# A dense expert stage that accumulates over three chunks instead of two

## The chip, the cores and the metric

The kernel runs on one core of one Trainium2 chip. Its time is the device time of one execution in microseconds (us). Of several runs the median is given. A profiled execution gives a trace: the start and duration of the instructions of TensorE (PE), VectorE (DVE), ScalarE (ACT) and GpSimd (POOL), the issues of transfers on the queues of SyncE (SP) and POOL, and what ended the idle time before an instruction.

## The reference

One layer of a diffusion backbone: attention and a linear recurrence, and behind them a mixer that retrieves experts. There are 256 context and 1024 latent tokens of 1024 channels, that is two and eight tiles of 128 tokens. The mixer is what the change touches. For each token, 8 heads choose 16 of 16384 experts each; an expert is a row of a table u and a row of a table v, both 16384 x 1024, float32.

```python
eid = jnp.take_along_axis(cid, pos, axis=-1)          # 128 experts of each token
g = jax.nn.softmax(best, axis=-1)
u = jnp.take(u_tab, eid, axis=0)
act = jax.nn.gelu(jnp.einsum('td,thkd->thk', xb, u))
vv = jnp.take(v_tab, eid, axis=0)
return jnp.einsum('thk,thkd->td', (g * act), vv)
```

## The kernel before

**Two ways through the mixer.** Four token tiles (both context tiles, two latent ones) are *gathered*, in `mix`: for each of the 128 experts of a tile's tokens, an indirect transfer issued by POOL brings a 128 x 1024 tile of u rows, a different expert for each token (L830), and DVE multiplies it by the tokens and sums (L833); then, 16 at a time, the v rows are gathered (L841) and DVE adds them, weighted, to the tile's sum (L847). That is 1024 gathered rows of 512 KB, in the names of the trace `row`.

The other six latent tiles are *dense*, in `dense`: all 16384 experts are computed for them, in 128 chunks of 128 experts, with the gate `gts` zero where a token did not choose an expert. For a chunk, `experts_in` (L696) multiplies the chunk's u rows with the tokens. For precision both factors are split into a high and a low part and three products are summed (`split`, L134 and L135: ACT writes the high part, DVE subtracts; `mm3`, L138 to L140). So the names `uh`, `ul`, `vh`, `vl`, `ah`, `al`. A chunk has 48 such matmuls of 384 columns on PE; ACT applies the GELU and gives `a` (128 x 768). DVE multiplies `a` by the gate (L761) and splits it. Then `add` (L724) multiplies with the chunk's v rows: 36 matmuls of 512 columns. Two of the six token tiles keep their sums in PSUM through all chunks (`res`, 12 matmuls of a chunk). The other four share two rotating PSUM tiles (`rot`, 24 matmuls of a chunk): a rot tile takes the products of the chunks of one *group* for one token tile and one half of the channels, ACT copies it to `q` (L741), and DVE adds `q` to the sum in SBUF (L742). A group is `GROUP` chunks.

**Early chunks.** For 44 of the 128 chunks `a` is computed ahead of the dense stage and stored in DRAM (`ad`), and loaded back in it (L758); there `ul` is computed by POOL. The other 84, the full chunks, do their u products in the dense stage. Early chunks come in pairs, so that of six chunks mostly two are early and four full.

**What sets the order.** A scheduler fixes the order of instructions on every engine when the program is built. The products of a group are added (`add`) when the first chunk of the next group has been prepared (L766, L767). The gathered rows are woven in by a credit: `tick` is called with a number of microseconds behind certain DVE instructions, the credit grows by it, and for each `D_STEP` = 2.0 us of it one more row is taken from the gather work. `paced` places the DVE instruction of that row right behind the DVE instruction of the tick, so where credit is given decides which DVE instructions stand between which rows. In the dense stage `a` times the gate and the split of `a` give `T_MUL` = 2.0 us each, and a group's adds share a sum that depends on whether the chunks beside them are early (`E_US`) or full (`PE_US`). Rows rotate through `N_ROW` tiles plus, in the dense stage, `N_MORE` more; a gather into a tile waits until DVE has read the row before in it.

The helper `row()` takes the tiles in turn; `order` and `ahead` (L689, L690) are the groups and whether they are early.

Of the kernel before, what the change touches and what calls it, by code (L numbers as in the profile page):

```python
# [9 lines left out]
F32 = mybir.dt.float32  # L10
F32R = mybir.dt.float32r
# [4 lines left out]
AF = mybir.ActivationFunctionType  # L16
# [5 lines left out]
P = 128  # L22
D = 1024
KD = D // P
S_CTX = 256
# [21 lines left out]
N_RES = 2  # L47
GROUP = 2
EARLY = 44
N_ROW = 4  # L50
N_MORE = 3

# [3 lines left out]
T_MUL = 2.0  # L56
E_US = 3.0
PE_US = 15.8

# [5 lines left out]
def body(ctx: ExitStack, tc: tile.TileContext, i, o):  # L65
# [622 lines left out]

    order = [range(c, c + GROUP) for c in range(0, P, GROUP)]  # L689
    ahead = [n * (EARLY // GROUP) % len(order) < EARLY // GROUP for n in range(len(order))]  # L690
    early = [c for cs, e in zip(order, ahead) if e for c in cs]
    ad = {c: dram.tile([P, TD], F32, name=f"ad{c}") for c in early}
    nb = -(-TD // 512)
    NB = TD // nb

    def experts_in(raw, nraw, c, hh, hl, out):  # L696

        u = raw.tile([P, KD, P], F32, name="u", bufs=nraw)
        nc.sync.dma_start(u, i["ut"][c])
        uh = eu.tile([P, KD, P], F32R, name="uh", bufs=2)  # L700
        ul = eu.tile([P, KD, P], F32R, name="ul", bufs=2)
        split(uh, ul, u, G if c in early else V)
        for b in range(nb):
            bs = slice(b * NB, (b + 1) * NB)
            p = eps.tile([P, NB], F32, name="u", bufs=2)
            for k in range(KD):
                mm3(p, (uh[:, k], ul[:, k]), (hh[:, k, bs], hl[:, k, bs]), k == 0, k == KD - 1)
            out(bs, p)

    def dense(tiles, hh, hl):  # L710
        with ExitStack() as es:
# [11 lines left out]

            def add(group, full):  # L724
                c0 = group[0][0]
                share = GROUP * (PE_US - 2 * T_MUL if full else E_US)
                for it in group:
# [3 lines left out]
                for x in range(N_RES, N_DENSE):  # L731
                    for hf in range(2):
                        p = ps.tile([P, 512], F32, name="rot", bufs=2)
                        for it in group:
                            product(p, x, hf, it, c0, c0 + GROUP - 1)
                        y = acc[x - N_RES][:, hf * 512:(hf + 1) * 512]
# [7 lines left out]
            last = None  # L744
            for cs, taken in zip(order, ahead):
                group = []
                for c in cs:
# [5 lines left out]
                    if c % 2 == 0:  # L753
                        gts = wk.tile([P, TD, 2], F32, name="gt", bufs=2)
                        nc.sync.dma_start(gts, gd[c // 2])
                    a = wk.tile([P, TD], F32, name="a", bufs=2)
                    if taken:
                        nc.sync.dma_start(a, ad[c])  # L758
                    else:
                        experts_in(wk, 2, c, hh, hl, lambda bs, p: A.activation(a[:, bs], p, AF.Gelu_apprx_tanh))  # L760
                    tick(T_MUL, V.tensor_tensor(a, a, gts[:, :, c % 2], op=OP.mult))  # L761
                    ah = wk.tile([P, TD], F32R, name="ah", bufs=GROUP + 1)
                    al = wk.tile([P, TD], F32R, name="al", bufs=GROUP + 1)
                    tick(T_MUL, split(ah, al, a))
                    group.append((c, ah, al, vh, vl))
                    if last:  # L766
                        add(last, not taken)  # L767
                        last = None
                last = group
            add(last, True)  # L770
            more.clear()
# [84 lines left out]
    with ExitStack() as ms:  # L856
# [4 lines left out]
        ctab = load("ctab", [P, NC], dt=I32)  # L861
        kc = load("kcT", [P, S_CTX])
        maskb = load("maskb", [P, 2, P], dt=BF16)
# [53 lines left out]
    with ExitStack() as fs:  # L917
# [3 lines left out]
        with ExitStack() as ks:  # L921
            kv = pool(ks, "lkv")
            kT = kv.tile([P, S_LAT], F32, name="kT")
            vv = kv.tile([P, N_LAT, P], F32, name="vv")
# [51 lines left out]
    with ExitStack() as es:  # L976
# [17 lines left out]
        for c in early:  # L994
            def keep_act(bs, p):
                a = vl.tile([P, NB], F32, name="a", bufs=2)
                A.activation(a, p, AF.Gelu_apprx_tanh)  # L997
                nc.sync.dma_start(ad[c][:, bs], a)
            experts_in(vl, 1, c, hha, hla, keep_act)
        phase("chB")  # L1000
# [96 lines left out]
```

## Time and profile before

| | |
|---|---|
| median of 3 runs | 3699.52 us (3689.12 to 3724.33) |
| profiled execution | 3691.55 us, its span 3689.7 us |
| mean granted clock of TensorE | 0.951 of 2.4 GHz |
| busy, PE / DVE / ACT / POOL | 3323.2 / 3082.3 / 1456.6 / 1728.7 us |
| busy share of the span | 90% / 84% / 39% / 47% |
| moved by DMA | 918.20 MB, 249 GB/s over the span |

The busy time is the time in which an engine executes; a busy share is an average over stages with different limits. The dense stage takes some 1880 us, about from 1760 to 3650 us of the span; ahead of it lie the modulation, the input projection, attention and recurrence, the output projection, the choice of experts, and the early chunks. A PE instruction's duration in the trace overlaps the next one's, so the distance of the starts is the time that one takes of the engine; for DVE the distance is some 0.08 us shorter than the duration.

### The profile page before, as it was taken

What the parts mean: (1) busy time and instruction counts of PE and PEld (TensorE: products, weight loads), DVE (VectorE), ACT (ScalarE), POOL (GpSimd) and SP (SyncE); (2) the same over time, 40 slices, a digit from 0 to 9 for tenths busy, and PEclk for the clock granted to TensorE, in tenths of its full rate; (3) what the DMA queues carried; (4) which work ended last, traced back from release to release, by engine and by line L of the source; (5) the groups of instructions that cost most, each with busy time, mean ns of one, the idle gap of its engine ahead of it and who ended that gap; (6) DMA issues with size and microseconds to landing.
All of it is one profiled execution on the core that took longest, in us unless ns stands there. A gap on an engine that the chain in (4) does not pass through costs nothing.

```text
span 3689.7 us, 48648 instructions
## 1 busy us (share of the span) xinstructions
PE 3323.2 (90%) x16982; PEld 2733.0 (74%) x16982; DVE 3082.3 (84%) x6710; ACT 1456.6 (39%) x2270; POOL 1728.7 (47%) x1162
## 2 busy tenths in 40 slices
PE   7888879888798988889899999989989999999995
PEld 4477654433598877779788888878878888887884
DVE  4549986767799999970699999989989998988898
ACT  5744645533211344542333333433333333333333
POOL 0012454556621121212366666656657666665663
PEclk8799989999899999999999999999999999999998
DMA  8342653568830256773799999988889998988885
GB/s 333 109 158 84 211 201 127 159 233 283 287 97 28 66 152 203 215 218 125 278 346 331 339 341 337 337 307 317 319 300 343 349 344 303 343 303 308 302 317 200
DMA packets 349142, 918.20 MB, mean 249 GB/s; under 512 B 29144, under 2 KB 150104, under 8 KB 345824
## 3 DMA queue, kind: packets, MB, share of 16 engines
q0 software_dynamic: 147456, 536.94, 41.3%
q1 hardware_dynamic: 201440, 378.16, 30.1%
q8 instruction: 133, 2.18, 0.2%
q14 instruction: 113, 0.93, 0.1%
HBM read 834.48 MB, written 80.50 MB: 248 GB/s over the span
## 4 chain that ended last, share of the span: by engine, by line
PE 33%; DVE 24%; issue 6%; DMA 3%; POOL 2%; ACT 1%; POOLq 0%; DVEq 0%; SPq 0%; ACTq 0%
PE u L140 6%; PE u L139 6%; PE u L138 6%; DVE row L833 4%; DVE acc L847 4%; PE rot L138 3%; PE rot L140 3%; PE rot L139 3%; DVE acc L742 2%; DVE oh L676 2%; PE res L138 2%; PE res L140 2%; PE res L139 2%; DVE oh L674 1%; DVE oh L677 1%
## 5 line engine op out<-in xcount | busy, mean ns | idle before, releaser
L830 POOL DMA_INDIRECT row<-in_peer_u,eid x512 | 732.6, 1431 | 571.1 <-DVE row L833 219.0
L841 POOL DMA_INDIRECT row<-in_peer_v,eid x512 | 716.3, 1399 | 493.1 <-DVE acc L847 226.9
L140 PE MATMUL u<-hh,ul 128*128 128x384 f32 x2048 | 709.2, 347 | 59.0 <-DVE ul L135 55.7
L138 PE MATMUL u<-hh,uh 128*128 128x384 f32 x2048 | 709.9, 347 | 6.2 <-ACT a L997 4.4
L139 PE MATMUL u<-hl,uh 128*128 128x384 f32 x2048 | 708.1, 346 | 0.0
L847 DVE SCALAR_TENSOR_TENSOR acc<-row,w,acc 128x1024 f32<-128x1024 f32 x508 | 655.9, 1291 | 25.8 <-DMA row<-in_peer_v,eid 24.3
L833 DVE SCALAR_TENSOR_TENSOR row<-row,h 128x1024 f32<-128x1024 f32 x512 | 623.9, 1233 | 56.6 <-DMA row<-in_peer_u,eid 56.4
L741 ACT ACTIVATE q<-rot 128x512 f32<-128x512 f32 x504 | 298.5, 596 | 479.7 <-PE rot L140 258.6
L140 PEld LDWEIGHTS u<-hh,ul 128*128 128x128 f32 x2048 | 396.7, 194 | 67.7 <-DVE ul L135 59.5
L138 PE MATMUL rot<-vh,ah 128*128 128x512 f32 x1024 | 408.5, 399 | 15.3 <-ACT q L741 14.9
L138 PEld LDWEIGHTS u<-hh,uh 128*128 128x128 f32 x2048 | 397.0, 194 | 14.2 <-ACT a L997 5.7
L139 PE MATMUL rot<-vl,ah 128*128 128x512 f32 x1024 | 400.9, 391 | 0.0
L139 PEld LDWEIGHTS u<-hl,uh 128*128 128x128 f32 x2048 | 396.7, 194 | 5.6
L140 PE MATMUL rot<-vh,al 128*128 128x512 f32 x1024 | 400.8, 392 | 0.0
L742 DVE TENSOR_TENSOR acc<-q,acc 128x512 f32<-128x512 f32 x504 | 342.7, 688 | 13.9 <-ACT q L741 12.4
L135 POOL TENSOR_TENSOR ul<-u,uh 128x1024 fp32r<-128x1024 f32 x44 | 120.6, 2741 | 427.1 <-ACT uh L134 404.2
L138 PE MATMUL mm<-hh,wh 128*128 128x256 f32 (+2 forms) x848 | 288.0, 340 | 12.9 <-ACT wh L134 12.9
L140 PE MATMUL mm<-hh,wl 128*128 128x256 f32 (+2 forms) x848 | 290.3, 343 | 7.4 <-POOL wl L135 4.7
L139 PE MATMUL mm<-hl,wh 128*128 128x256 f32 (+2 forms) x848 | 285.6, 337 | 0.0
L135 DVE TENSOR_TENSOR vl<-v,vh 128x1024 fp32r<-128x1024 f32 x128 | 156.3, 1221 | 120.4 <-DMA gt<-gd 115.9
L134 ACT ACTIVATE uh<-u 128x1024 fp32r<-128x1024 f32 x128 | 135.7, 1061 | 294.2 <-PE u L139 235.5
L138 PEld LDWEIGHTS rot<-vh,ah 128*128 128x128 f32 x1024 | 193.3, 189 | 74.3 <-ACT q L741 36.3
(260 smaller groups left out, 6079.1 us busy)
## 6 DMA issues: line engine op xcount, KB each, us to landing
u<-in_ut SPq DMA_DIRECT2D x128, 512.0 KB
v<-in_peer_v SPq DMA_DIRECT2D x128, 512.0 KB
gd<-stg SPq DMA_DIRECT2D x12, 4096.0 KB
gt<-gd SPq DMA_DIRECT2D x64, 768.0 KB
w<-in_w_mod SPq DMA_DIRECT2D x24, 1024.0 KB
ad<-a SPq DMA_DIRECT2D x88, 192.0 KB
a<-ad SPq DMA_DIRECT2D x44, 384.0 KB
w<-in_w_query SPq DMA_DIRECT2D x32, 512.0 KB
```

The costliest lines, as they stand in the source:

```text
L134: A.activation(hi, src, AF.Copy)
L135: return (eng or V).tensor_tensor(lo, src, hi, op=OP.subtract)
L138: T.matmul(out, lhs[0], rhs[0], start=first, stop=False)
L139: T.matmul(out, lhs[0], rhs[1], start=False, stop=False)
L140: T.matmul(out, lhs[1], rhs[0], start=False, stop=last)
L676: V.tensor_tensor(oh.rearrange(four, j=2), o2.rearrange(four, j=2), pairs(gh, ts), op=OP.mult)
L741: A.activation(q, p, AF.Copy)
L742: tick(share / (2 * (N_DENSE - N_RES)), V.tensor_tensor(y, q, y, op=OP.add))
L830: G.indirect_dma_start(out=u, out_offset=None, in_=i["peer_u"], in_offset=bass.IndirectOffsetOnAxis(ap=eid[:, k:k + 1], axis=0))
L833: V.scalar_tensor_tensor(u, u, 1.0, h2, op0=OP.mult, op1=OP.mult, accum_out=act[:, j:j + 1])
L841: G.indirect_dma_start(out=v, out_offset=None, in_=i["peer_v"], in_offset=bass.IndirectOffsetOnAxis(ap=eid[:, k:k + 1], axis=0))
L847: V.scalar_tensor_tensor(acc, v, w[:, j:j + 1], acc, op0=OP.mult, op1=OP.add)
```

## The change

A group is three chunks (`GROUP` 3): 43 groups, the last one of two. The early chunks are the same 44, but a group may now hold early and full chunks: of six chunks, in two groups, one group is full and the other has two early chunks and a full one. The share of credit of a group's adds is the sum over the chunks that are prepared beside it, with 1.2 us for an early and 17.0 - 2 x 2.0 = 13.0 for a full one. There are `N_MORE` = 1 more tiles for rows in the dense stage, five in all, where there were seven. The tile `a` has one buffer in place of two, and `ah` and `al` are taken ahead of it; `vh`, `vl`, `ah` and `al` have four buffers (GROUP + 1), three before. `kcT`, the cached keys, is loaded into a pool of the latent stage when that opens, not at the start.

```diff
--- before.py
+++ after.py
@@ -45,17 +45,17 @@
 
 
 N_RES = 2
-GROUP = 2
+GROUP = 3
 EARLY = 44
 N_ROW = 4
-N_MORE = 3
+N_MORE = 1
 
 F_STEP = 1.9
 D_STEP = 2.0
 STEP = {"spread": 1e9, "ret": 4.0}
 T_MUL = 2.0
-E_US = 3.0
-PE_US = 15.8
+E_US = 1.2
+PE_US = 17.0
 
 NORM = "AAGV"
 G_SCALE = 32768.0
@@ -686,16 +686,14 @@
             nc.sync.dma_start(gd[:, :, c0:c0 + SB, :].rearrange("g p t j -> p g t j"), stg)
 
 
-    order = [range(c, c + GROUP) for c in range(0, P, GROUP)]
-    ahead = [n * (EARLY // GROUP) % len(order) < EARLY // GROUP for n in range(len(order))]
-    early = [c for cs, e in zip(order, ahead) if e for c in cs]
+    early = [c for c in range(P) if c // 2 * (EARLY // 2) % (P // 2) < EARLY // 2]
+    order = [range(c, min(c + GROUP, P)) for c in range(0, P, GROUP)]
     ad = {c: dram.tile([P, TD], F32, name=f"ad{c}") for c in early}
     nb = -(-TD // 512)
     NB = TD // nb
 
-    def experts_in(raw, nraw, c, hh, hl, out):
-
-        u = raw.tile([P, KD, P], F32, name="u", bufs=nraw)
+    def experts_in(u, c, hh, hl, out):
+
         nc.sync.dma_start(u, i["ut"][c])
         uh = eu.tile([P, KD, P], F32R, name="uh", bufs=2)
         ul = eu.tile([P, KD, P], F32R, name="ul", bufs=2)
@@ -721,9 +719,9 @@
                 cols = slice(hf * 512, (hf + 1) * 512)
                 mm3(p, (ah[:, xs], al[:, xs]), (vh[:, cols], vl[:, cols]), c == first, c == last)
 
-            def add(group, full):
+            def add(group, beside):
                 c0 = group[0][0]
-                share = GROUP * (PE_US - 2 * T_MUL if full else E_US)
+                share = sum(E_US if c in early else PE_US - 2 * T_MUL for c in beside)
                 for it in group:
                     for x in range(N_RES):
                         for hf in range(2):
@@ -732,7 +730,7 @@
                     for hf in range(2):
                         p = ps.tile([P, 512], F32, name="rot", bufs=2)
                         for it in group:
-                            product(p, x, hf, it, c0, c0 + GROUP - 1)
+                            product(p, x, hf, it, c0, group[-1][0])
                         y = acc[x - N_RES][:, hf * 512:(hf + 1) * 512]
                         if c0 == 0:
                             A.activation(y, p, AF.Copy)
@@ -742,7 +740,7 @@
                             tick(share / (2 * (N_DENSE - N_RES)), V.tensor_tensor(y, q, y, op=OP.add))
 
             last = None
-            for cs, taken in zip(order, ahead):
+            for cs in order:
                 group = []
                 for c in cs:
                     v = wk.tile([P, D], F32, name="v", bufs=2)
@@ -753,21 +751,22 @@
                     if c % 2 == 0:
                         gts = wk.tile([P, TD, 2], F32, name="gt", bufs=2)
                         nc.sync.dma_start(gts, gd[c // 2])
-                    a = wk.tile([P, TD], F32, name="a", bufs=2)
-                    if taken:
+                    ah = wk.tile([P, TD], F32R, name="ah", bufs=GROUP + 1)
+                    al = wk.tile([P, TD], F32R, name="al", bufs=GROUP + 1)
+                    a = wk.tile([P, TD], F32, name="a")
+                    if c in early:
                         nc.sync.dma_start(a, ad[c])
                     else:
-                        experts_in(wk, 2, c, hh, hl, lambda bs, p: A.activation(a[:, bs], p, AF.Gelu_apprx_tanh))
+                        experts_in(wk.tile([P, KD, P], F32, name="u", bufs=2), c, hh, hl,
+                                   lambda bs, p: A.activation(a[:, bs], p, AF.Gelu_apprx_tanh))
                     tick(T_MUL, V.tensor_tensor(a, a, gts[:, :, c % 2], op=OP.mult))
-                    ah = wk.tile([P, TD], F32R, name="ah", bufs=GROUP + 1)
-                    al = wk.tile([P, TD], F32R, name="al", bufs=GROUP + 1)
                     tick(T_MUL, split(ah, al, a))
                     group.append((c, ah, al, vh, vl))
                     if last:
-                        add(last, not taken)
+                        add(last, cs)
                         last = None
                 last = group
-            add(last, True)
+            add(last, order[-1])
             more.clear()
             spare = [wk.tile([P, KD, P], F32, name="u", bufs=2).rearrange("p k e -> p (k e)") for _ in range(2)]
             spare += [wk.tile([P, D], F32, name="v", bufs=2) for _ in range(2)]
@@ -859,7 +858,6 @@
         chan = load("chan", [P, 4, 15])
         sink = load("sink", [P, NH])
         ctab = load("ctab", [P, NC], dt=I32)
-        kc = load("kcT", [P, S_CTX])
         maskb = load("maskb", [P, 2, P], dt=BF16)
         identb = load("identb", [P, P], dt=BF16)
         nsink = const.tile([P, NH], F32, name="nsink")
@@ -920,6 +918,7 @@
         gy = fo.tile([P, 4, S_LAT], F32, name="gy")
         with ExitStack() as ks:
             kv = pool(ks, "lkv")
+            kc = load("kcT", [P, S_CTX], kv)
             kT = kv.tile([P, S_LAT], F32, name="kT")
             vv = kv.tile([P, N_LAT, P], F32, name="vv")
             phase("lproj")
@@ -996,7 +995,7 @@
                 a = vl.tile([P, NB], F32, name="a", bufs=2)
                 A.activation(a, p, AF.Gelu_apprx_tanh)
                 nc.sync.dma_start(ad[c][:, bs], a)
-            experts_in(vl, 1, c, hha, hla, keep_act)
+            experts_in(vl.tile([P, KD, P], F32, name="u"), c, hha, hla, keep_act)
         phase("chB")
         for t in gt[N_CTX:]:
             combine(cb, *found[t], t, 1)
```

On DVE, in the dense stage, at the end of one group's adds where full chunks are prepared beside it. Before (row: a gathered row, acc<-q: an add of a group, L833 the product of a gathered u row, L135 a split):

```order
L833 SCALAR_TENSOR_TENSOR row,act<-row,h_26906 128x1024
L742 TENSOR_TENSOR acc_16142<-q,acc_16142 128x512
L833 SCALAR_TENSOR_TENSOR row,act<-row,h_26906 128x1024
L742 TENSOR_TENSOR acc_16142<-q,acc_16142 128x512
L833 SCALAR_TENSOR_TENSOR row,act<-row,h_26906 128x1024 x2
L742 TENSOR_TENSOR acc_16143<-q,acc_16143 128x512
L833 SCALAR_TENSOR_TENSOR row_29508,act<-row_29508,h_26906 128x1024
L742 TENSOR_TENSOR acc_16143<-q,acc_16143 128x512
L833 SCALAR_TENSOR_TENSOR row_29521,act<-row_29521,h_26906 128x1024
L833 SCALAR_TENSOR_TENSOR row_29524,act<-row_29524,h_26906 128x1024
L135 TENSOR_TENSOR vl<-v,vh 128x1024
L135 TENSOR_TENSOR ul<-u,uh 128x1024
```

With the change, at such a place (L740 is the add, L832 and L846 the gathered rows of u and v, L762 the gate):

```order
L832 SCALAR_TENSOR_TENSOR row_26034,act<-row_26034,h_21763 128x1024
L740 TENSOR_TENSOR acc_16143<-q,acc_16143 128x512
L832 SCALAR_TENSOR_TENSOR row,act<-row,h_21763 128x1024 x2
L135 TENSOR_TENSOR vl<-v,vh 128x1024
L832 SCALAR_TENSOR_TENSOR row,act<-row,h_21763 128x1024 x2
L762 TENSOR_TENSOR a<-a,gt 128x768
L836 TENSOR_TENSOR w<-w,gw_9879 128x16
L135 TENSOR_TENSOR vl<-v,vh 128x1024
L846 SCALAR_TENSOR_TENSOR acc<-row_26078,w,acc 128x1024
L135 TENSOR_TENSOR al<-a,ah 128x768
L846 SCALAR_TENSOR_TENSOR acc<-row,w,acc 128x1024
L135 TENSOR_TENSOR ul<-u,uh 128x1024
```

Before, 14 rows and the 8 adds stand ahead of ul in such a place, and now 21 rows and 8 adds, with two vl, a product with the gate and an al between them.

On SP, the loads where a pair of early chunks begins (a<-ad is the load of an early chunk's a, v, u and gt are the chunks' rows and gates). Before:

```order
L699 DMA u<-in_ut 128x1024
L758 DMA a<-ad_131 128x768
L749 DMA v<-in_peer_v 128x1024
L755 DMA gt<-gd 128x1536
L758 DMA a<-ad_132 128x768
L749 DMA v<-in_peer_v 128x1024 x2
L755 DMA gt<-gd 128x1536
L749 DMA v<-in_peer_v 128x1024 x2
```

With the change:

```order
L753 DMA gt<-gd 128x1536
L758 DMA a<-ad_131 128x768
L747 DMA v<-in_peer_v 128x1024
L758 DMA a<-ad_132 128x768
L747 DMA v<-in_peer_v 128x1024 x2
L753 DMA gt<-gd 128x1536
L747 DMA v<-in_peer_v 128x1024
L753 DMA gt<-gd 128x1536
```

The second load of a stands two places behind the first instead of three, and now goes into the tile of the first; behind it are the loads of v and gt for the next chunks.

## Rows read from the trace of the kernel before

**Rows 1.** Busy times, and a group: busy, mean ns of one, idle before it.

```profile
PE 3323.2 (90%) x16982; PEld 2733.0 (74%) x16982; DVE 3082.3 (84%) x6710; ACT 1456.6 (39%) x2270; POOL 1728.7 (47%) x1162
...
L742 DVE TENSOR_TENSOR acc<-q,acc 128x512 f32<-128x512 f32 x504 | 342.7, 688 | 13.9 <-ACT q L741 12.4
```

**Rows 2.** Windows: length, busy us of PE, PEld, DVE, ACT, POOL; clock, DMA share, GB/s.

```profile
1760.00:3660.00 1900.00, 1806.59 (x8638) 1584.55 (x8638) 1732.55 (x2225) 696.82 (x1057) 1160.47 (x801) 0.97 0.89 320
2100.00:2200.00 100.00, 100.00 (x490) 88.19 (x489) 98.86 (x131) 40.64 (x62) 67.05 (x47) 1.00 0.95 353
2400.00:2500.00 100.00, 83.98 (x375) 71.82 (x374) 83.67 (x107) 30.90 (x47) 52.05 (x38) 0.92 0.85 304
```

**Rows 3.** PE's waits, 1810 to 3650 us: us in total, times, longest.

```profile
PE u L140 <- DVE ul L135: 55.7, 9, 9.0
PE rot L138 <- ACT q L741: 13.9, 14, 7.8
PE res L138 <- ACT ah L134: 13.8, 7, 4.0
```

**Rows 4.** DVE's waits in the same stretch.

```profile
DVE ul L135 <- ACT uh L134: 81.6, 21, 9.4
DVE row L833 <- DMA row<-in_peer_u,eid: 21.5, 14, 5.3
DVE a L761 <- DMA a<-ad: 14.5, 4, 11.2
```

**Rows 5.** PE's timeline: start, duration, instruction, [idle before it <- releaser].

```profile
3250.03 0.40 PE L139 MATMUL rot<-vl,ah 128*128 128x512 f32 x1
...
3254.13 0.39 PE L140 MATMUL rot<-vh,al 128*128 128x512 f32 x1
3263.47 0.69 PE L140 MATMUL u<-hh,ul 128*128 128x384 f32 x1 [8.95 <-DVE ul L135]
...
3264.28 0.52 PE L139 MATMUL u<-hl,uh 128*128 128x384 f32 x1
...
3269.08 0.52 PE L139 MATMUL u<-hl,uh 128*128 128x384 f32 x1
...
3269.80 0.34 PE L139 MATMUL u<-hl,uh 128*128 128x384 f32 x1
...
3271.89 0.34 PE L138 MATMUL u<-hh,uh 128*128 128x384 f32 x1
```

**Rows 6.** DVE's timeline at the same place.

```profile
3242.05 0.68 DVE L742 TENSOR_TENSOR acc<-q,acc 128x512 f32<-128x512 f32 x1
3242.65 1.28 DVE L847 SCALAR_TENSOR_TENSOR acc<-row,w,acc 128x1024 f32<-128x1024 f32 x1
3243.85 0.68 DVE L742 TENSOR_TENSOR acc<-q,acc 128x512 f32<-128x512 f32 x1
...
3259.92 1.22 DVE L833 SCALAR_TENSOR_TENSOR row<-row,h 128x1024 f32<-128x1024 f32 x1
...
3261.07 1.22 DVE L135 TENSOR_TENSOR vl<-v,vh 128x1024 fp32r<-128x1024 f32 x1
3262.20 1.21 DVE L135 TENSOR_TENSOR ul<-u,uh 128x1024 fp32r<-128x1024 f32 x1
...
3275.08 1.23 DVE L135 TENSOR_TENSOR ul<-u,uh 128x1024 fp32r<-128x1024 f32 x1 [9.40 <-ACT uh L134]
```

**Rows 7.** POOL's timeline: gathers issued.

```profile
1878.08 1.21 POOL L830 DMA_INDIRECT row<-in_peer_u,eid  x1 [0.56 <-DVE rs_s L150]
...
1886.04 1.68 POOL L830 DMA_INDIRECT row<-in_peer_u,eid  x1 [2.50 <-DVE row L833]
...
3025.01 1.68 POOL L830 DMA_INDIRECT row<-in_peer_u,eid  x1 [6.58 <-DVE acc L847]
```

**Rows 8.** DVE's timeline: the instructions that read two of these rows.

```profile
1884.53 1.23 DVE L833 SCALAR_TENSOR_TENSOR row<-row,h 128x1024 f32<-128x1024 f32 x1 [2.44 <-DMA row<-in_peer_u,eid]
...
3032.92 1.22 DVE L833 SCALAR_TENSOR_TENSOR row<-row,h 128x1024 f32<-128x1024 f32 x1 [3.79 <-DMA row<-in_peer_u,eid]
```

## The prediction

> **What bounds the kernel now.** The table of busy times and the windows come first. TensorE (PE) is busy for 3323.2 us of the span and VectorE (DVE) for 3082.3 [rows 1]. The dense stage lies in the stretch from 1760 to 3660 us: PE 1806.59, DVE 1732.55, ScalarE (ACT) 696.82 of 1900 us, clock 0.97 [rows 2]. The change acts in this stretch alone. Its windows are of two kinds. In 2100 to 2200 PE is busy for all 100 us at clock 1.00, with DVE at 98.86 and 353 GB/s; in 2400 to 2500 PE has 83.98 at clock 0.92. So PE is the bound, DVE is full right behind it, and the stage loses time in a few spots.
>
> PE's floor: in the PE timeline 18 rot or res matmuls start in 4.10 us (3250.03 to 3254.13), 0.228 us each, and 12 u matmuls in 2.09 us (3269.80 to 3271.89; one row there counts two), 0.174 us each [rows 5]. All 128 chunks have 36 of the first kind and the 84 full chunks 48 of the second: 128 x 36 x 0.228 + 84 x 48 x 0.174 = 1050 + 702 = 1752 us. The stretch holds 1900, of which some 15 are its run-in and end, so about 130 us are lost to idle PE and to its lower clock.
>
> Where: of PE's waits, u for DVE's ul has 55.7 us in nine times, then rot for ACT's q 13.9 and res for ACT's ah 13.8 [rows 3]. One of the nine is in the timelines: PE's last rot starts at 3254.13, its next u only at 3263.47, after 8.95 us of waiting; from 3264.28 to 3269.08 15 matmuls take 4.80 us, 0.32 each, the 1.2 GHz level after the idle time, and at 3269.80 the 0.174 is back [rows 5]. A spot so costs its idle time and some 16 x (0.32 - 0.174) = 2.4 us of slow matmuls: 55.7 + 9 x 2.4 = 77 us for the nine. Meanwhile DVE never paused: rows and adds up to 3261.07, then vl, and ul at 3262.20 [rows 6]. Too many gathered rows stood ahead of ul in its queue. Then DVE in its turn waited 9.40 us for ACT's uh [rows 6]; such waits sum to 81.6 us [rows 4], and are the other side of the same spots.
>
> **The change, part by part.** *Accumulating over three chunks* takes 504 - 336 = 168 q copies from ACT and as many adds from DVE. An add holds DVE's queue for 0.60 us (3242.05 to 3242.65) [rows 6], and there were 504 [rows 1]: 101 us of DVE. ACT, busy for 37% of the stage, gives nothing by it. PE executes the same matmuls. So the 101 us count only at the spots above: had they all vanished, the gain would be 130 us, the bound on that side (3692 - 130 = 3562).
>
> *The order.* Where three full chunks lie beside a group's adds, 39 us of credit (3 x 13) are spread over eight adds, and a gathered row is taken for each 2.0. In DVE's order 21 rows and 8 adds now stand ahead of the next ul, where the stalled spots before had 14 and 8; half of the 43 groups, 21, are of this kind. That is 21 x 1.17 + 8 x 0.60 = 29.4 us of DVE (rows 1.20 with the add, 1.15 by the other line's step from 3259.92 to 3261.07) [rows 6], and with two vl, an a and an al among them some 33.4; PE has 36 res, 72 rot and 48 u to do before it must have ul, 108 x 0.228 + 48 x 0.174 = 33.0 us, so this is near even. Counted burst by burst from the two orders, from the last add to ul on DVE against what PE still has, before comes out short in the nine stalled spots and by 63 us (measured 55.7), and after in six by 27 us, with some ten more within 1.3 us of short. If rows were never late, the new idle time would be 27 us in 6 spots, 27 + 6 x 2.4 = 41 against 77.
>
> *Five buffers for rows instead of seven.* The trace has no burst of 21, so the price comes from how long a gather takes from its issue on GpSimd to the DVE instruction that waits for it: 1878.08 to 1884.53 is 6.45 us, 3025.01 to 3032.92 is 7.91 [rows 7, 8]. These are waits that ended with the landing. From the end of a DVE row, 1884.53 + 1.23 = 1885.76, to the issue that it releases, 1886.04, are 0.3 us. With 1.2 us of reading, a buffer comes round in 8.0 to 9.4 us, a row each 1.59 to 1.88 us through five. DVE could take one each 29.4 / 21 = 1.40. The first five are there; the other 16 come late by 16 x 0.19 = 3.0 to 16 x 0.48 = 7.7 us. With seven buffers and 14 rows the same latencies give 1.14 to 1.34 against (14 x 1.17 + 4.8) / 14 = 1.51: never late, as before has just 21.5 us of such waits in 1840 us [rows 4]. I take 7.0 us of latency, nearer the lower row, since with five tiles fewer transfers share the DMA engines: 8.5 / 5 = 1.70, 16 x 0.30 = 4.8 us late per burst. In the 16 bursts without slack PE pays all: 16 x 4.8 = 77 us. In the five others DVE has room, and I cost them at nothing; were that cover gone, it is 5 x 4.8 = 24 more, or 38 at the upper end.
>
> *One tile for a.* The load of the second early chunk's a now waits until DVE has split the first, 22 times. Behind it on SyncE's queue stand two v loads and a gt load, and DVE has one row and two vl in between (some 3.5 us). Late loads of a cost DVE 14.5 us in four waits before, the longest of 11.2 [rows 4]. The bounds are nothing, as PE has a whole group of rot and res ahead there, and 22 x (7.2 - 3.5) = 81 us, when a load takes the rows' mean of the two above, 7.2, and nothing covers it. I take 5 us: DVE's wait is met by the adds it no longer has, 16 for 24 in six chunks, 8 x 0.60 = 4.8 us.
>
> *The rest.* ah and al taken ahead of a, and the u tile as an argument, move nothing by themselves. The number of early chunks stays 44, and the row counts are 222 ahead of the stage and 802 in it, in both. kcT is loaded one stage later and is read later still, in the attention: nothing; if late, once a load of a few us.
>
> **The sum**, against the profiled execution's 3691.55 us: away go 77 us; new are 27 + 77 of idle PE, and 16 spots x 2.4 = 38 of slow matmuls, and 5 for a: 147 - 77 = **+70 us, 3762 us**. The median of the three runs, 3699.52, lies 8 us above the profiled one; the verdict is against it, +1.7%. With the latency's two rows the sum is 3692 + 16 x 3.0 + 27 + 38 + 5 - 77 = 3733 and 3692 + 123 + 38 + 27 + 38 + 81 - 77 = 3922, the latter with every cover gone.
>
> **The rivals.** (1) *Faster: rows come in time.* A gather that comes in under 5.5 us makes 0.3 + 5.5 + 1.2 = 7.0, 1.40 per row: no lag. That is where this case decides. Against it, both gathers shown take longer [rows 7, 8], and the stage moves 320 GB/s where its full windows move 353 [rows 2]. For it, the full windows have seven rows in flight, and five would queue less. Then 41 replaces 77: 3692 - 36 = 3656; if the ten near-even bursts also gain from the freed DVE, down to 3562, say 3640. The Trainium skill ("DMA: Bandwidth & Descriptors", the anatomy of a gpsimd-path DMA) fits one such transfer as 2.0 us plus bytes over 436 GB/s, an estimate of 3.2 us for a 512 KB row; by it a buffer would come round in 4.7 us, 0.94 us per row, and this rival would hold. The trace differs: 6.45 and 7.91 us [rows 7, 8], and the measurement decides. By the rows alone the case needs a latency 0.95 us under the shorter of them: chance 0.20.
> (2) *No change: gain and loss cancel*, at a latency near 6.0 us: 7.5 / 5 = 1.50, 16 x 0.10 = 1.6 us late, 16 x 1.6 = 26; 27 + 26 + 20 (8 spots) + 5 - 77 = 0: 3692. Chance 0.17.
> (3) *The single a tile decides.* If SyncE's queue stands behind the load of a, v and gt come late too; then each pair costs PE 3.7 us and a slow restart of 2.4: 22 x 6.1 = 134 on top of the lag at its lower end (3733 - 5): 3862. Chance 0.08. For it: four such waits in the trace though the tile was double; against it, PE has a group's 24.6 us of res and rot in hand there.
>
> The forecast has 0.55. A measurement of this kernel can tell 1%, some 37 us, from no change. Of the faster rival 0.15 lies under 3663 us and 0.05 above; the cancelling one is "same", as is 0.03 of the forecast. So faster 0.15, same 0.25, slower 0.60. The range: 3645 leaves out some 0.1 below, and 3850 some 0.08 above, with rival (3) mostly outside.
>
> **What would show it.** In the profile after: the group of q copies and adds 336 each, DVE's busy time less by about 168 x 0.688 = 116 us [rows 1], PE's the same within its clock. DVE's waits of row for its gather rise from 21.5 to some 80 to 150 us, in bursts with all five tiles empty. PE's waits for ul become more and shorter, or pass to res and rot, whose q and ah stand behind late rows. The stage's share of DMA falls below 0.89. Waits of DVE for a<-ad number some 20. I am wrong if row waits stay under 40 us (then rival 1), or if PE's waits are for DVE instructions with no row wait ahead of them: then the order, and not the buffers, is the cost.

## The result: slower by 4.8%, more than twice the forecast

| | before | changed |
|---|---|---|
| median of the runs | 3694.32 us (4 runs) | 3881.79 us (3859.09 to 3883.09, 4 runs) |
| ratio | | 1.0482, 95% interval 1.0449 to 1.0514 |
| span of the profiled execution | 3689.7 us | 3879.9 us |
| mean granted clock | 0.951 | 0.935 |

The direction was the forecast's, the size was not: some 178 us by the ratio against 70, and the time lies above the range of 3645 to 3850.

The page of the changed kernel, its busy times and the group of the adds, as in [rows 1]:

```profile
PE 3378.9 (87%) x16982; PEld 2765.6 (71%) x16982; DVE 2998.6 (77%) x6542; ACT 1361.8 (35%) x2102; POOL 1677.7 (43%) x1162
...
L740 DVE TENSOR_TENSOR acc<-q,acc 128x512 f32<-128x512 f32 x336 | 234.3, 698 | 29.1 <-ACT q L739 28.9
```

The adds are 336 and their time 108 us less. The saving that was bought has arrived, and the kernel is slower all the same. The dense stage, one window (columns as in [rows 2]):

```profile
1760.00:3850.00 2090.00, 1858.23 (x8640) 1616.64 (x8640) 1647.08 (x2056) 602.24 (x887) 1120.28 (x803) 0.94 0.84 293
```

It has the same matmuls in 190 us more. DVE, idle for 167 of 1900 us before, is now idle for 443 of 2090 us, and the transfers have become fewer per second, 293 for 320 GB/s: no engine is full, all of them wait. For whom, PE's waits say (1810 to 3840 us, against [rows 3]):

```profile
PE res L138 <- ACT ah L134: 115.7, 29, 15.7
PE rot L138 <- ACT q L739: 46.0, 23, 6.0
PE u L138 <- ACT a L761: 38.8, 12, 8.6
PE res L140 <- DVE al L135: 8.9, 14, 2.2
PE u L140 <- DVE ul L135: 6.7, 4, 2.5
```

The nine waits for ul are all but gone, 55.7 us to 6.7, below the 27 us in six spots of the forecast. In their place stand waits for ah, for q and for a, all written by ACT. In all PE's listed waits rise from 90 to 220 us, and the granted clock falls from 0.97 to 0.94 of the stage, 57 to 125 us of clock withheld, some of it while PE was idle anyway: 130 us and up to 68 more.

ACT is not busy. The chain of waits in one stretch of the stage, 2100 to 2195 us (start, length, what), shows what it waits for:

```profile
2105.38 1.23 DVE vl L135
2106.67 6.46 DMA v<-in_peer_v
2113.15 1.06 ACT vh L134
2114.21 0.74 ACT ah L134
...
2123.78 0.96 DVE al L135
2124.76 9.60 DMA a<-ad
...
2136.45 0.95 DVE al L135
...
2142.09 5.17 DMA row<-in_peer_u,eid
2147.29 1.23 DVE row L832 x2
...
2157.26 1.15 DVE vl L135
2158.47 7.07 DMA v<-in_peer_v
```

Four transfers of 5.2 to 9.6 us stand bare in 60 us. Three of them begin just when DVE has let go of a tile: vl ends and a v load starts, al ends and the load of the next a starts. These are not late transfers, they are transfers that could not start. The fourth, a gather, comes out of the same standstill: while DVE waits for a, it reads no row, and POOL waits 7.34 us for a row tile; then it issues one gather behind the other ("issue" means that the engine waited for nothing).

```profile
2136.80 1.41 POOL L829 DMA_INDIRECT row<-in_peer_u,eid  x1 [7.34 <-DVE acc L846]
...
2142.09 1.49 POOL L829 DMA_INDIRECT row<-in_peer_u,eid  x1 [0.31 <-issue]
2143.88 1.44 POOL L829 DMA_INDIRECT row<-in_peer_u,eid  x1 [0.30 <-issue]
```

What the load of a does to PE is in the timelines of the same stretch (DVE, ACT, PE):

```profile
2134.38 0.96 DVE L762 TENSOR_TENSOR a<-a,gt 128x768 f32<-128x768 f32 x1 [6.12 <-DMA a<-ad]
...
2135.37 0.84 ACT L134 ACTIVATE ah<-a 128x768 fp32r<-128x768 f32 x1 [11.83 <-DVE a L762]
2136.12 1.06 ACT L739 ACTIVATE q<-rot 128x512 f32<-128x512 f32 x2
...
2136.75 0.80 PE L138 MATMUL rot<-vh,ah 128*128 128x512 f32 x1 [3.71 <-ACT q L739]
```

ACT's copies to q stand behind ah, ah behind the product with the gate, and that behind the load; PE's rot waits for a PSUM tile that q has not yet emptied.

DVE's waits (against [rows 4]) and ACT's line for vh say the same of the whole:

```profile
DVE row L832 <- DMA row<-in_peer_u,eid: 112.0, 88, 5.9
DVE ul L135 <- ACT uh L134: 105.2, 22, 9.6
DVE vl L135 <- ACT vh L134: 70.6, 20, 11.1
DVE a L762 <- DMA a<-ad: 42.7, 15, 6.1
```

```profile
L134 ACT ACTIVATE vh<-v 128x1024 fp32r<-128x1024 f32 x128 | 132.2, 1055 | 246.7 <-DMA v<-in_peer_v 235.5 <-PE rot L140 9.5
```

In the kernel before that line reads:

```profile
L134 ACT ACTIVATE vh<-v 128x1024 fp32r<-128x1024 f32 x128 | 133.4, 1055 | 48.3 <-PE rot L140 41.3 <-DMA v<-in_peer_v 6.3
```

ACT waits 235.5 us for v where it waited 6.3, and ah stands behind vh in its queue. The groups of three make this wait: e8 below, the changed kernel with groups of two and the same tiles, has 6.2 us of it.

```profile
L134 ACT ACTIVATE vh<-v 128x1024 fp32r<-128x1024 f32 x128 | 132.6, 1054 | 39.2 <-PE rot L140 32.4 <-DMA v<-in_peer_v 6.2
```

### The profile page after: what moved, and what is told of

Same layout as the page of the kernel before. It is cut to its first block, busy times and chain, and to the rows that moved or that the text cites. A ratio compares the mean times of both kernels' runs of the same rounds, so it can differ in the third digit from the quotient of the medians.

```text
span 3879.9 us, 48253 instructions
## 1 busy us (share of the span) xinstructions
PE 3378.9 (87%) x16982; PEld 2765.6 (71%) x16982; DVE 2998.6 (77%) x6542; ACT 1361.8 (35%) x2102; POOL 1677.7 (43%) x1162
## 4 chain that ended last, share of the span: by engine, by line
issue 19%; POOL 13%; DMA 8%; DVE 7%; PE 4%; ACT 1%; POOLq 0%; DVEq 0%; SPq 0%; ACTq 0%
POOL row L840 7%; POOL row L829 6%; DMA row<-in_peer_u,eid 4%; DVE acc L846 2%; DVE row L832 1%; DMA v<-in_peer_v 1%; DMA a<-ad 1%; DMA row<-in_peer_v,eid 1%; PE u L140 1%; PE u L138 1%; PE u L139 1%; DVE acc L740 1%; DVE al L135 1%; DVE a L762 1%; DVE vl L135 0%
## 5 line engine op out<-in xcount | busy, mean ns | idle before, releaser
L829 POOL DMA_INDIRECT row<-in_peer_u,eid x512 | 702.5, 1372 | 683.1 <-DVE row L832 373.2
L840 POOL DMA_INDIRECT row<-in_peer_v,eid x512 | 700.7, 1368 | 611.7 <-DVE acc L846 347.2
L138 PE MATMUL u<-hh,uh 128*128 128x384 f32 x2048 | 710.6, 347 | 46.3 <-ACT a L761 38.8
L832 DVE SCALAR_TENSOR_TENSOR row<-row,h 128x1024 f32<-128x1024 f32 x512 | 627.8, 1235 | 145.4 <-DMA row<-in_peer_u,eid 143.8
L846 DVE SCALAR_TENSOR_TENSOR acc<-row,w,acc 128x1024 f32<-128x1024 f32 x508 | 654.7, 1289 | 29.0 <-DMA row<-in_peer_v,eid 26.8
L739 ACT ACTIVATE q<-rot 128x512 f32<-128x512 f32 x336 | 199.4, 595 | 505.8 <-PE rot L140 317.7
L138 PE MATMUL res<-vh,ah 128*128 128x512 f32 x512 | 222.9, 436 | 126.1 <-ACT ah L134 125.9
L135 POOL TENSOR_TENSOR ul<-u,uh 128x1024 fp32r<-128x1024 f32 x44 | 119.4, 2715 | 448.0 <-ACT uh L134 425.2
L135 DVE TENSOR_TENSOR vl<-v,vh 128x1024 fp32r<-128x1024 f32 x128 | 155.9, 1220 | 189.7 <-DMA gt<-gd 119.1
L740 DVE TENSOR_TENSOR acc<-q,acc 128x512 f32<-128x512 f32 x336 | 234.3, 698 | 29.1 <-ACT q L739 28.9
```

Of the source, the lines that this page charges most:

```text
L135: return (eng or V).tensor_tensor(lo, src, hi, op=OP.subtract)
L138: T.matmul(out, lhs[0], rhs[0], start=first, stop=False)
L739: A.activation(q, p, AF.Copy)
L740: tick(share / (2 * (N_DENSE - N_RES)), V.tensor_tensor(y, q, y, op=OP.add))
L829: G.indirect_dma_start(out=u, out_offset=None, in_=i["peer_u"], in_offset=bass.IndirectOffsetOnAxis(ap=eid[:, k:k + 1], axis=0))
L832: V.scalar_tensor_tensor(u, u, 1.0, h2, op0=OP.mult, op1=OP.mult, accum_out=act[:, j:j + 1])
```

## The experiments

Ratios are to the kernel before, with 95% intervals. "Stretches" counts, in DVE's order, the places with 29 or more gathered rows between one ul and the next.

| run | groups | credits | row tiles | a | v | ratio | stretches |
|---|---|---|---|---|---|---|---|
| before | 2 | old | 7 | 2 | 2 | 1 | 9 |
| e1 | 2 | old | 5 | 2 | 2 | 1.0275 (1.0231 to 1.0319) | 12 |
| e2 | 2 | old | 7 | 1 | 2 | 1.0363 (1.0317 to 1.0410) | 6 |
| e3 | 2 | old | 5 | 1 | 2 | 1.0586 (1.0533 to 1.0639) | 6 |
| e4 | 2 | new | 7 | 2 | 2 | 0.9889 (0.9844 to 0.9934) | 2 |
| e8 | 2 | new | 5 | 1 | 2 | 1.0370 (1.0338 to 1.0402) | 0 |
| the change | 3 | new | 5 | 1 | 2 | 1.0482 (1.0449 to 1.0514) | 7 |
| e11 | 3 | old | 5 | 1 | 2 | 1.0432 (1.0380 to 1.0485) | 5 |
| e6 | 3 | new | 5 | 2 | 2 | 1.0352 (1.0309 to 1.0394) | 8 |
| e7 | 3 | new | 7 | 1 | 2 | 1.0316 (1.0281 to 1.0351) | 3 |
| e5 | 3 | new | 7 | 2 | 2 | 1.0213 (1.0179 to 1.0247) | 10 |
| e9 | 3 | new | 7 | 2 | 3 | 1.0142 (1.0092 to 1.0192) | 10 |
| e16 | 3 | new | 7 | 3 | 3 | 1.0167 (1.0130 to 1.0204) | 9 |
| e14 | 3 | T_MUL 4 | 7 | 2 | 3 | 1.0244 (1.0227 to 1.0261) | 15 |
| e13 | 3 | old | 7 | 2 | 3 | 1.0061 (1.0042 to 1.0081) | 10 |
| e17 | 3 | old | 7 | 3 | 3 | 1.0044 (1.0027 to 1.0061) | 7 |
| e12 | 2 | new | 8 | 2 | 2 | 0.9830 (0.9783 to 0.9877) | 2 |
| e15 | 2 | PE_US 16 | 8 | 2 | 2 | 0.9888 (0.9861 to 0.9914) | 0 |

**One part of the change at a time, in the kernel before.** e1 takes two row tiles away (the first edit), e2 the second a (the second), e3 both, e4 changes the credits alone (the third).

```diff
-N_MORE = 3
+N_MORE = 1
...
-                    a = wk.tile([P, TD], F32, name="a", bufs=2)
+                    a = wk.tile([P, TD], F32, name="a")
...
-E_US = 3.0
-PE_US = 15.8
+E_US = 1.2
+PE_US = 17.0
```

> The kernel before (groups of two, two tiles for a, old credits) with N_MORE 1: five tiles for gathered rows instead of seven, nothing else. Theory R (the five row tiles cost most of the 177 us): at the forecast's 8.5 us a round a row comes each 1.70 us against DVE's 1.51 in a burst of 14, so DVE's waits for rows rise from 21.5 to over 80 us and the ratio to before is 1.02 to 1.04. Theory S (the single tile for a costs most): under 1.015.

> The kernel before with one tile for a instead of two, nothing else. Theory S: the second early chunk's load goes out only behind the al of the first and takes 9 to 10 us, as in the changed kernel (issue 2124.76, DVE's a at 2134.38), and a full chunk's GELU waits for the al of the chunk before; 22 pairs x 5 us and the waits of u for a: ratio 1.025 to 1.045. Theory R and the forecast (5 us in all): under 1.01.

> The kernel before with one tile for a and five tiles for rows, groups of two and old credits as before. If the two tiles' costs are what the change lost, and the groups of three and the new credits gave or took little: ratio 1.04 to 1.06, near the changed kernel's 1.048. If the groups of three or the credits are the cost: under 1.02. If the two waits fall in the same idle time, the sum is less than e1 and e2 together.

> The kernel before with the new credits alone (E_US 1.2, PE_US 17.0): fewer rows beside early chunks, more beside full ones. Theory P (the crowding of rows beside full chunks is the cost): the bursts ahead of ul grow from 14 to 15 or 16 rows and PE's waits for ul from 55.7 to 100 us or more, ratio 1.02. Theories R and S: within 0.985 to 1.01, since the credit of six chunks stays about the same (24 + 47.2 + 6 = 77.2 before, 24 + 52 + 2.4 = 78.4 now).

Neither theory R nor S holds alone: five row tiles cost 2.75% (101 us), one a 3.6% (134 us), both 5.9%. The waits of DVE in e1 (1810 to 3650 us) show the rows, up from 21.5 [rows 4], and those of e2 the loads of a, up from 14.5:

```profile
DVE row L833 <- DMA row<-in_peer_u,eid: 83.9, 68, 5.8
...
DVE a L761 <- DMA a<-ad: 11.9, 2, 9.9
```

```profile
DVE a L761 <- DMA a<-ad: 56.2, 13, 5.7
DVE row L833 <- DMA row<-in_peer_u,eid: 49.6, 29, 6.3
```

In e2, with seven row tiles, rows too come late more often (49.6), probably for the reason seen in the chain above: while DVE stands still for a, POOL gets no tile to gather into. In PE's waits of e2 (1810 to 3600 us) the price appears at the adds, for q, 13.9 before [rows 3], not where a is read:

```profile
PE rot L138 <- ACT q L741: 80.9, 39, 7.1
PE u L140 <- DVE ul L135: 52.3, 8, 9.3
```

e4 was a surprise: theory P expected a loss, and the new credits gain 1.1% (41 us). PE's waits for ul in it, from the same view:

```profile
PE u L140 <- DVE ul L135: 27.1, 5, 9.5
```

55.7 in nine became 27.1 in five. The order tells why: before, nine places have 33 to 37 rows and 22 to 24 adds between one ul and the next, and each of PE's nine waits is for the ul behind one of them; under the new credits two such places are left, with 30 and 37 rows. (In e1 there are twelve, and PE's twelve waits for ul are behind them.) So in groups of two it is not how many rows stand beside a group's adds that makes PE wait for ul, it is mostly how long DVE goes without one; three waits of e4 and three of e2's nine are behind shorter stretches. In groups of three the count says little of it: PE waits for other things first, and the changed kernel has seven such stretches and 6.7 us of waits for ul.

**The parts together.** e8 is the changed kernel with groups of two.

```diff
-GROUP = 3
+GROUP = 2
```

> The changed kernel with groups of two (GROUP 2) and all else as changed: five row tiles, one a, new credits. Against the changed kernel's 1.048 it shows what the groups of three gave or took under its own tiles. Theory A: 1.045 to 1.05 (e3's 1.0586 less e4's 0.011). Theory G: under 1.035. Theory F, if the saved adds count at all: above 1.055.

1.037, between the ranges of theories A and G; none of the three holds. So the sum runs: credits -1.1% (e4), the tiles for rows and a +4.8% on top (e8 over e4), groups of three +1.1% on top (the change over e8). Groups of three, which save 168 adds, cost 41 us here. (kcT's move and the new place of ah and al were not tried by themselves; both are in e8, and in e12, the fastest run.)

**Groups of three with the tiles given back.** The memory has no room for it, so the low part of the tokens is left out behind the choice of experts:

```diff
-            hla = hx.tile([P, KD, TD], F32R, name="hl")
             hs = ctx.enter_context(ExitStack())
             hx = pool(hs, "hxb")
+            hla = hx.tile([P, KD, TD], F32R, name="hla")
...
-            experts_in(vl.tile([P, KD, P], F32, name="u"), c, hha, hla, keep_act)
+            experts_in(vl.tile([P, KD, P], F32, name="u"), c, hha, hha, keep_act)
...
-    dense(dt, hha, hla)
+    dense(dt, hha, hha)
```

> The changed kernel with nothing altered but the low part of the tokens left out in the dense stage and for the early chunks (the high part stands in for it), as in e5 to e7 and e9. It shows what that replacement does to the time by itself: nothing, 1.043 to 1.053 (the changed kernel 1.048), if PE's matmuls take the same time whatever their operands are; if less, e5 to e7 are too low by the difference.

1.0492 (1.0437 to 1.0546), against 1.0482: the replacement itself changes no time that can be told, and the runs with it can be read. e5 to e7 add `N_MORE = 3` and a's `bufs=2`, both or one.

> The changed kernel (groups of three, new credits) with both tiles given back: two tiles for a and seven for rows. The memory comes from the low part of the tokens, which is left out: in the dense stage and for the early chunks the products with it use the high part in its place, with the same matmuls. It shows what the groups of three are worth by themselves; e4 (groups of two, new credits, same tiles) is 0.989. Theory A (costs add: rows 101, a 135, credits -41 us, groups about 0): ratio 0.98 to 1.00. Theory F (the 101 us of adds saved on VectorE come out once the waits are gone): 0.96 to 0.98. Theory G (21 rows between two ul and three v loads in a row cost as much as the adds saved, or more): 1.01 to 1.03, with waits of vl for vh and PE's of res for ah left.

> As e5, but with five tiles for rows: the changed kernel with a second tile for a (low part of the tokens left out as in e5). Against the changed kernel (1.048) it shows the single a's share: theory A: ratio near 1.012 (1.048 less 0.036); theory G: the a tile's wait lies in idle time that the bursts cause anyway, 1.025 to 1.04.

> As e5, but with one tile for a: the changed kernel with seven tiles for rows (low part of the tokens left out as in e5). Theory A: 1.048 less 0.028, near 1.02; the forecast's lag of 77 us and more for five tiles: likewise 1.02 to 1.027. Theory G: 1.03 to 1.04.

Theory G holds in all three. Given back alone, the second a is worth 1.3% and the two row tiles 1.7%, both 2.7%; in groups of two both were worth 4.8%. With both, groups of three are at 1.021 where groups of two with the same tiles and credits stand at 0.989 (e4): 3.2% for the groups alone. The waits of PE and DVE in e5 (1810 to 3600 us) are those of the changed kernel, only shorter:

```profile
PE res L138 <- ACT ah L134: 74.9, 23, 8.7
PE rot L138 <- ACT q L739: 22.2, 15, 4.2
PE u L138 <- ACT a L761: 18.6, 5, 5.5
...
PE u L140 <- DVE ul L135: 7.1, 4, 3.0
...
DVE row L832 <- DMA row<-in_peer_u,eid: 78.3, 51, 7.4
```

The waits for v are left too: ACT's vh waits 150.9 us.

```profile
L134 ACT ACTIVATE vh<-v 128x1024 fp32r<-128x1024 f32 x128 | 132.4, 1056 | 161.8 <-DMA v<-in_peer_v 150.9 <-PE rot L140 9.8
```

e9 has three tiles for v.

```diff
-                    v = wk.tile([P, D], F32, name="v", bufs=2)
+                    v = wk.tile([P, D], F32, name="v", bufs=3)
```

> As e5 (groups of three, new credits, two a, seven row tiles, low part of the tokens left out), with three tiles for v instead of two. In e5 ACT still waits 137.6 us in 36 times for a v load (6.3 us in the kernel before), and ah stands behind vh in its queue, for which PE's res waits 74.9 us. Theory V (three chunks are split in a row, and the third v load can only go out behind the first vl): those waits fall under 50 us and PE's res for ah under 40, ratio 0.995 to 1.01. Theory B (the burst of 21 rows itself, whose late rows and a loads hold up DVE): ratio stays at 1.015 to 1.025.

```profile
L134 ACT ACTIVATE vh<-v 128x1024 fp32r<-128x1024 f32 x128 | 130.8, 1053 | 18.1 <-PE rot L140 10.9 <-DMA v<-in_peer_v 5.8
```

The wait for v is gone, and with it 0.7%, a difference at the edge of the noise (the two intervals just meet): theory V is right on the wait and wrong on its worth (0.995 to 1.01), since PE's res still waits 64.1 us for ah; theory B misses its range by a hair. Behind that DVE waits for rows and for loads of a (1810 to 3560 us):

```profile
DVE row L832 <- DMA row<-in_peer_u,eid: 81.3, 46, 8.4
DVE a L762 <- DMA a<-ad: 56.0, 14, 10.7
```

**What is left of it: the credits.** e11 is the changed kernel with the old credits; e13 and e14 are e9 with the old credits and with `T_MUL = 4.0`.

> The changed kernel with the old credits (E_US 3.0, PE_US 15.8). Theory A (costs add; the new credits gave 41 us in groups of two): 1.055 to 1.065. Theory B (beside three full chunks the new credits crowd 21 rows, and 3 x 11.8 = 35.4 us of credit crowd only 19, with more beside early chunks): 1.035 to 1.045.

> e9 (groups of three, two a, seven row tiles, three v tiles, low part of the tokens left out) with the old credits (E_US 3.0, PE_US 15.8). In DVE's order e9 has 11 stretches with 33 or more rows and 16 adds between one ul and the next; this has 7, and four of 29 to 30. Theory B (these stretches are what is left of the cost of groups of three): ratio 1.000 to 1.010, under e9's 1.014. If the total of the credit counts and not its place: 1.014 or more, as the old credits cost 41 us in groups of two.

> e9 with T_MUL 4.0: each product with the gate and each split of a gives two rows instead of one, and the adds beside three full chunks 27 us of credit instead of 39. The rows are spread more evenly over the DVE instructions, but the scheduler then puts 37 to 39 rows and 16 adds between two ul in 11 places one behind the other, 9 of them in the first half of the stage. Theory B (the stretches between ul count): 1.014 to 1.035, slower than e9. Theory C (the crowding of rows at the adds counts): 0.99 to 1.008, faster than e9.

e11 lies in theory B's range, and theory A falls; it is not told apart from the change (the intervals meet). With tiles enough the old credits are better by 0.8% (e13, in theory B's range), where in groups of two they were worse by 1.1%: a set of credits belongs to one order. e14, in which the rows lie more evenly among DVE's instructions, is slower by 1.0%, and theory C falls. It has 15 long stretches for e9's ten, and PE waits 22.7 us for ul (1810 to 3560 us) for e9's 8.8. e13 has ten as well (the expectation counted them wrongly), but leaves 42 rows behind the last ul, e9 30, and so has fewer in the stage; its waits for rows are 55.0 us, e9's 81.3. The count of stretches alone does not explain e13.

> e9 (groups of three, new credits, seven row tiles, three v tiles, low part of the tokens left out; 1.014) with three tiles for a instead of two. In e9 DVE still waits 56.0 us for loads of a, and PE's res 64.1 us for ah, which is made from a. Theory L (a group's early chunks are prepared one behind the other, so two tiles are too few for them): DVE's wait for a under 20 us, ratio 1.000 to 1.009. Theory B (rows: 81.3 us of late rows in stretches of up to 38 rows): 1.010 to 1.018.

> e16 with the old credits (e13 with three tiles for a; e13 1.006). If groups of three with tiles enough and rows better placed do bring the 101 us of adds that they save: under 0.99. If the adds are worth nothing on the path: 0.995 to 1.005. Theory L: 0.005 to 0.015 under e13. Theory B: within 0.005 of e13.

A third a changes nothing (1.0167 and 1.0044, within the intervals of e9 and e13), and theory L falls: in e16 the loads of a still cost DVE 59.0 us (before, 14.5), so it is not the number of tiles that holds them. The trace of e16 shows what does in its four longest waits, 41 of the 59 us. One of them, on SP's queue and on DVE:

```profile
2964.00 7.51 SPq L747 DMA_DIRECT2D v<-in_peer_v  x2
2972.32 1.45 SPq L697 DMA_DIRECT2D u<-in_ut  x2
2973.82 1.34 SPq L758 DMA_DIRECT2D a<-ad  x2
...
2984.60 1.91 DVE L762 TENSOR_TENSOR a<-a,gt 128x768 f32<-128x768 f32 x2 [11.22 <-DMA a<-ad]
```

The load of a goes out right behind loads of v and u, which SP could issue only when DVE had done its vl and ul, and lands some 10 us later. What another order on SP's queue would bring was not tried. What is shown is that no run with groups of three, with 101 us of adds less on DVE, came under the kernel before.

**A version that beats both.** Groups of two need less memory; with the new credits, two tiles for a and kcT's move, eight row tiles fit (e12); e15 is e12 with `PE_US = 16.0`.

```diff
-GROUP = 3
+GROUP = 2
-N_MORE = 1
+N_MORE = 4
-                    a = wk.tile([P, TD], F32, name="a")
+                    a = wk.tile([P, TD], F32, name="a", bufs=2)
```

> A version meant to beat both: the changed kernel's credits, early chunks and kcT move, but groups of two, two tiles for a and eight tiles for rows (the memory of the smaller groups). e4 with one row tile more: its waits for rows, 38.4 us, should fall to 20 or less and its ratio of 0.989 to 0.975 to 0.985. If rows were no longer late on a path that counts: 0.989.

> e12 (groups of two, two a, eight row tiles) with PE_US 16.0 instead of 17.0. In DVE's order no stretch between two ul has more than 27 rows, where e12 has (37, 24 adds) and (30, 24); but 48 rows are left behind the last ul, some 15 to 20 more than in e12. Theory B: PE's waits for ul, 23.8 us, go to under 8 and the stage ahead of its end gains 20 to 40 us; the rows left over give 20 to 30 us back: ratio 0.972 to 0.985 (e12 0.983).

e12 is 3637.75 us, 0.983, the fastest of all; its interval meets e4's 0.989 and e15's. Its waits for rows are 20.3 us, as expected. e15 missed its range: without long stretches its stage is nearly free of stalls (PE waits 5.5 us for ul, e12 23.8), but the rows left over fill the end. The windows of e15 and then of e12:

```profile
1760.00:3550.00 1790.00, 1763.12 (x8582) 1552.94 (x8583) 1685.65 (x2164) 689.83 (x1041) 1126.37 (x773) 0.99 0.90 331
3550.00:3650.00 100.00, 14.47 (x60) 10.43 (x58) 74.48 (x105) 15.74 (x28) 46.28 (x34) 0.59 0.62 212
```

```profile
1760.00:3550.00 1790.00, 1723.20 (x8333) 1518.67 (x8332) 1671.63 (x2150) 666.36 (x1010) 1169.22 (x784) 0.98 0.91 332
3550.00:3650.00 100.00, 75.48 (x361) 64.93 (x359) 86.71 (x118) 37.88 (x62) 37.05 (x23) 0.90 0.55 206
```

Up to 3550 us e15 has done 249 matmuls more than e12; in the last 100 us its PE has 14 us of work and its DVE still 74, of which 42 are gathered rows (e12: 26). What was won in the stage was given back behind it.

## Why the forecast had the sign and missed the size

- **The bound and the nine stalls: right.** PE's waits for ul fell from 55.7 to 6.7 us. That the saved adds count at most at such places fits too: no run with groups of three came under the kernel before.
- **The new idle time of the order, 27 us: the step that failed.** The sum had 27 us of waits for ul and 14 of slow matmuls where the nine stalls had 77, a gain of 36 us if rows came in time; what res, rot and u wait for on ACT it put at nothing (the signs at its end name res and rot, behind late rows; the sum has no term for them). e5, with both tiles given back, is 79 us slower than the kernel before: PE waits 7.1 us for ul there, but 74.9 for ah, 22.2 for q and 18.6 for a (before, 13.8, 13.9 and none in the list). From -36 to +79 are 115 us, as much as the whole miss (178 - 70 = 108).
- **Three chunks split one behind the other: the part of it that is shown.** The prediction named the two v loads behind the load of a, and priced neither. Two tiles for v are too few when three v are split in a row: ACT's wait for v went from 6.3 to 235.5 us, and PE's res for ah from 13.8 to 115.7. A third tile brings 26 us (e9 over e5, at the edge of the noise).
- **The tiles: right in sum, by luck.** Rows were put at 77 us and the slow matmuls of ten more spots, 24, and a at 5: 106. Both given back bring 99 us (e5 against the change); but alone the rows bring 62 (e7) and a 48 (e6). Two errors cancel.
- **One tile for a: mis-sized.** It was put at 5 us, between 0 and 81, "as PE has a whole group of rot and res ahead there" and because DVE had 4.8 us to spare. The runs: 134 us in groups of two (e2), 48 us on top of the other waits in the changed kernel (e6). PE's work in hand did not cover it, since that work needs q and acc<-q, which stand behind the waiting a in ACT's and DVE's queues (the timelines above). And one tile binds the full chunks too: their GELU writes it, and PE's u waits for ACT's a (38.8 us in twelve times; with two tiles, e5, 18.6 are left, and e2 lists none, so one tile is not its only cause).
- **The burst of 21 rows and the five tiles: the number came out, the mechanism is half of it.** Waits for rows were forecast at 80 to 150 us and came to 112.0, in groups of two to 83.9 (e1). But with seven tiles, where the same sum has a row each 8.5 / 7 = 1.21 us against 1.40 and so none late, groups of three still wait 78.3 us (e5). The sum lacks a limit: where POOL waits for nothing, one gather follows the other after 1.80 us (the median of 278 in the changed kernel; 2142.09 and 2143.88 above), which is slower than the 1.40 that DVE can take in a burst, whatever the tiles. Of the changed kernel's 94 late rows of u and v in the stage (116 us), 53 (56 us) come from gathers that had waited for no tile. No run tests this limit by itself.
- **The credits: taken as nothing, and they gained 41 us** in groups of two (e4), by the same stretches.
- **The rivals.** The third, with 3862 us, came nearest in time, but not by its mechanism: a alone is worth 48 us and not 134, and v comes late with two tiles for a as well (150.9 us in e5). The faster one needed gathers under 5.5 us; the late gathers of the changed kernel took 4.2 to 9.8 us from issue to landing, 6.0 in the middle, and the one in the chain 5.17. The Trainium skill's fit ("DMA: Bandwidth & Descriptors", the anatomy of a gpsimd-path DMA), an estimate of 3.2 us for a row, is not borne out: 5.17 us at a DMA share of 0.84.
- **Not right:** DVE's busy time fell by 84 us and not by 116. The adds are 108 less; the durations of all DVE instructions add up to 124 less, but 41 us less of them overlap, since waits pull them apart.

What stays open: the last 1.4% of groups of three with tiles enough (e9), some 52 us, of which the old credits take 0.8% back. PE waits there for ah, and DVE for rows and for loads of a; which of the two counts, and what POOL's issues and SP's order have in it, is not shown.

## What to carry to other kernels

A tile with one buffer is a wait for the whole length of its next load, put into the queue of every engine that touches it; price it by that length and by what is queued behind it there, not by the engine that has work in hand. Before paying memory for fewer instructions, ask which tiles it takes, and price each tile by itself in the kernel as it stands: here two row tiles and one a cost 5.9% (e3), and 168 adds gave nothing. When a group grows, look through the waits of the bound engine one by one, not only at the one that is longest now: here the wait for ul went, and those for ah, q and a came. And to find where an engine will starve, count what stands between two instructions that feed it, not how much stands beside one; in groups of two that found all nine waits, in groups of three other waits came first.

## What the runs showed of the hardware

A single transfer takes long in this stage, though the rate is not at its highest: from issue to landing 384 KB of a took 9.60 us, and 512 KB of v 6.46 and 7.07 us, while the stage moved 293 GB/s, less than the 353 of the full windows [rows 2]. A slower stage did not make the single transfer short: three loads of a in the kernel before took 9.28 to 10.81 us. And GpSimd (POOL) has a pace of its own: some 1.45 us for the issue of one gather, and 1.80 us (the median of 278) from one to the next when it waits for nothing.
